# A row of c through TensorE, and the opening's vector work shared out anew, in a one-core encoder layer

## The chip, the cores and the metric

The kernel runs on one core of a Trainium2 chip. The metric is the device time of one execution in microseconds, given as the median over runs; before the change it is 1217.26 us (three runs, 1215.96 to 1217.44). One further execution was profiled. All work is in float32; the large products use pairs of fp32r numbers, a high part and a rest, and take three matrix products each.

## The reference

One layer of an encoder trunk over x (1024 rows, width 1024), with a condition vector c (1024):

```
mod = silu(c) @ w_ada + b_ada                       # six vectors of 1024
h   = rmsnorm(x) * norm_mix_w * (1 + sc_m) + sh_m
P   = h @ w_in                                      # z, xbc, dt, q, k, v
x   = x + g_m * (concat(ssd(z, xbc, dt), attention(q, k, v)) @ w_out)
h   = rmsnorm(x) * norm_ffn_w * (1 + sc_f) + sh_f
x   = x + g_f * conv_ffn(h)
out = rmsnorm(x)
```

rmsnorm(x) is x * (mean(x^2) + 1e-6)^(-1/2) for each row. silu(c) is c * sigmoid(c), computed as 0.5c * (1 + tanh(0.5c)). This case concerns only the first three lines, for the first 768 columns of w_in that the kernel treats (q, k and v of the first two pairs of heads).

## The kernel before

The opening loads eight tiles of x, 128 rows each, in two halves of four (hh = 0 and 1), and treats the width of h in eight blocks of 128 (kt = 0 to 7).

- c comes as a [128, 1024] array in which every row is c. It is loaded whole into rowa (L120), and its silu is made on all 128 partitions, by VectorE, ScalarE and VectorE (L191 to L193).
- Each x tile goes through norm1 (L296): ScalarE squares it and sums the rows (L268, into a scratch tile "junk" of one buffer), GpSimd adds epsilon and takes the power -1/2 (rstd, L116 and L117), and VectorE scales the tile in place (L301). Tiles 0 to 3 are loaded at once; tiles 4 to 7 are loaded from inside the loop over kt, behind a one-column copy on VectorE (L345) that depends on the scale of block kt (XL = 3, 4, 5, 6).
- In the first pass (hh = 0) each block kt needs its scale and shift. mod_col (L131) loads 128 rows of the transposed w_ada and VectorE multiplies them with rowa and sums (L134, "reduction"), once for the scale and once for the shift. mod_scale (L200) then makes the block's scale amix from two one-column instructions (L202, L204); mod_shift (L207) makes the shift bmix from one (L208).
- The block's weights (128 by 768) are loaded into one of two buffers (raws); ScalarE rounds them to a high part wsh and VectorE makes the rest wsl (split, L80; L85, L86).
- h_block (L270) makes the block's part of h: TensorE transposes four x tiles into PSUM (L273), ScalarE applies scale and shift into a float32 tile tmp (named hf, L276), VectorE rounds it to the high part hi (named hH, L277) and makes the rest lo (hL, L278).
- TensorE multiplies block kt into four accumulators for q and k (first_qk, L307, through mm3, L75: high by high L76, rest by high L77, high by rest L78) and two for v (first_v, L312; "vps"). Blocks 0 to 5 go in at once, blocks 6 and 7 in a tail after the loop, each product in a fixed order (those matmuls appear under L58). In that tail the first two blocks of the second half of x are transposed too.
- The second pass (hh = 1) uses the same weights again; it needs x tiles 4 to 7, no more reductions and no more weights.

Each engine issues its instructions in an order that a planner fixes when the program is built, from durations that it assumes; nothing is reordered at run time, so an instruction that waits holds back all behind it on its engine. DMAs are issued from SyncE's queue, also in order. The reductions' data have two buffers for the scale and two for the shift, the weights two: each load waits for the reduction or the weight rest two blocks earlier.

Of the kernel before, what the change touches and what calls it, by code (L numbers as in the profile page):

```python
# [10 lines left out]
F32 = mybir.dt.float32  # L11
F32R = mybir.dt.float32r
AF = mybir.ActivationFunctionType
ALU = mybir.AluOpType
PSUM = bass.MemoryType.PSUM

P = 128
D = 1024
# [6 lines left out]
EPS = 1e-6  # L25
# [9 lines left out]
B_ADA, NMIX, NFFN, SNW, SCW, SCB, FCW, DTB, ALOG, DSK = (  # L35
    0, 48, 56, 64, 68, 100, 108, 240, 248, 256)
NPK = 264
SH_M, SC_M, G_M, SH_F, SC_F, G_F = (8 * i for i in range(6))
# [26 lines left out]
def tile_block(ctx: ExitStack, tc: tile.TileContext, x, crep, pk, w_ada, w_first, w_ft, w_z,  # L65
               w_out, w_up, w_down, bias, fnw, out, dbg=None):
    nc = tc.nc
    V, A, T = (InOrder(tc, e) for e in (nc.vector, nc.scalar, nc.tensor))
    G = nc.gpsimd
# [19 lines left out]
    const = ctx.enter_context(tc.tile_pool(name="const", bufs=1))  # L89
    rw = ctx.enter_context(tc.tile_pool(name="rw", bufs=1, reuse_waits="tile"))  # L90
    es_l = ExitStack()
    wu = es_l.enter_context(tc.tile_pool(name="wu", bufs=2, reuse_waits="tile"))
    dram = ctx.enter_context(tc.tile_pool(name="dram", bufs=1, space=bass.MemoryType.DRAM))

    pkt = const.tile([P, 272], F32, name="pkt")[:, 0:NPK]
    rows_ = rw.tile([P, 2, D], F32, tag="w0", name="rows")
    rowa, rowb = rows_[:, 0, :], rows_[:, 1, :]
    raws = rw.tile([P, 2, D], F32, tag="w1", name="raws")
    ident = const.tile([P, P], F32, name="ident")
    mhalf = const.tile([P, 8], F32, name="mhalf")  # L100
    modc = const.tile([P, 48], F32, name="modc")
# [4 lines left out]
    def stat(n=1):  # L106
        if stc[0] + n > 64:
            stc[0] = 0
        a = st1[:, stc[0]:stc[0] + n]
        stc[0] += n  # L110
        return a

    def rstd(ms, eps=EPS):
        n = ms.shape[-1]
        r = stat(n)
        G.tensor_scalar(ms, ms, eps, 1.0, op0=ALU.add, op1=ALU.mult)  # L116
        G.tensor_tensor(r, ms, mhalf[:, 0:n], ALU.pow)  # L117
        return r

    nc.sync.dma_start(rowa, crep)  # L120
    nc.sync.dma_start(pkt, pk)
    make_identity(nc, ident)
    G.memset(mhalf, -0.5)
# [45 lines left out]
    def c4(ap):  # L169
        return ap.rearrange("p (a b) -> p a b", a=4)  # L170
# [11 lines left out]
    s0 = es_0.enter_context(tc.tile_pool(name="s0", bufs=1, side="right"))  # L182
    ps0b = es_0.enter_context(tc.tile_pool(name="ps0b", bufs=1, space=PSUM, side="right"))
    es_0a = ExitStack()
    ps0 = es_0a.enter_context(tc.tile_pool(name="ps0", bufs=1, space=PSUM))
# [2 lines left out]
        return qkp.tile([P, 1024], dt, tag="qk", name="qk")  # L188


    V.tensor_scalar(rowb, rowa, 0.5, None, op0=ALU.mult)  # L191
    A.activation(rowa, rowb, AF.Tanh)
    V.scalar_tensor_tensor(rowa, rowa, 1.0, rowb, op0=ALU.add, op1=ALU.mult)  # L193

    amix = const.tile([P, 16], F32, name="amix")[:, 0:8]
    bmix = const.tile([P, 8], F32, name="bmix")
# [3 lines left out]
    def mod_scale(dst, sc, nw, kt, n=1):  # L200
        t = stat(n)
        V.tensor_tensor(t, modc[:, sc + kt:sc + kt + n], pkt[:, B_ADA + sc + kt:B_ADA + sc + kt + n],  # L202
                        ALU.add)
        V.scalar_tensor_tensor(dst[:, kt:kt + n], t, 1.0, pkt[:, nw + kt:nw + kt + n],  # L204
                               op0=ALU.add, op1=ALU.mult)
# [6 lines left out]
    A.activation(na, pkt[:, ALOG:ALOG + 8], AF.Exp)  # L212
    V.tensor_scalar(pkt[:, SNW:SCW], pkt[:, SNW:SCW], 512.0 ** 0.5, None, op0=ALU.mult)


    qk = {}

# [52 lines left out]
    def h_block(hh, kt):  # L270
        tps = ps0.tile([P, 512], F32, tag="tp0", bufs=2, name="tp0")
        for j in range(4):
            T.transpose(tps[:, j * P:(j + 1) * P], xts[4 * hh + j][:, kt * P:(kt + 1) * P], ident)  # L273
        tmp = s0.tile([P, 512], F32, tag="hf", bufs=2, name="hf")
        hi, lo = ht(hh, kt)
        i = A.activation(tmp, tps, AF.Identity, scale=amix[:, kt:kt + 1], bias=bmix[:, kt:kt + 1])  # L276
        V.tensor_copy(hi, c4(tmp))  # L277
        return i, V.tensor_tensor(lo, c4(tmp), f32(hi), ALU.subtract)  # L278

    wsh = s0.tile([P, KT, 768], F32R, name="wsh")  # L280
# [7 lines left out]
    xts = []  # L288
# [7 lines left out]
    def norm1(st):  # L296
        ms = stat()
        junk = s0.tile([P, D], F32, tag="junk", name="junk")
        norm_to(xts[st], junk, ms)
        r = rstd(ms)  # L300
        V.tensor_scalar(xts[st], xts[st], r, None, op0=ALU.mult)  # L301

    for st in range(4):
        norm1(st)
# [24 lines left out]
    for hh in range(2):  # L329
        accs = [(ps0, ps0b)[n // 2].tile([P, 512], F32, tag="acc0", bufs=2, name="acc0") for n in range(4)]  # L330
        vps = [psv.tile([P, 2, 256], F32, tag=t, bufs=1, name="vps") for t in ("acc", "pv")]
        split_at = KT - (2, 4)[hh]
        tail = range(split_at, KT)
        for kt in range(KT):
            if hh == 0:
                mod_col(SC_M + kt, wu.tile([P, 1024], F32, tag="wh", name="adat"))
                mod_scale(amix, SC_M, NMIX, kt)
                mod_col(SH_M + kt, adw[:, kt % 2, :])
                mod_shift(bmix, SH_M, kt)
                t = raw_tile(768)  # L340
                nc.sync.dma_start(t, w_first[kt])
                split(wsh[:, kt, :], ws_lo(kt), t, A, V)
                for st in range(4, NT):
                    if XL[st - 4] == kt:
                        V.tensor_copy(xts[st][:, 0:1], amix[:, kt:kt + 1])  # L345
                        nc.sync.dma_start(xts[st], x[st * P:(st + 1) * P, :])
                        norm1(st)
            if hh == 0 or kt > 1:
                i = h_block(hh, kt)
            if hh == 1 and kt == 3:  # L350
                wpin = i
            if kt < split_at:
                for n in range(4):
                    first_qk(accs[n], n, hh, (kt,))
                first_v(vps, hh, (kt,))
        T.on, T.last = True, None
        if hh == 0:
            for kt in range(2):
                T.on = False
                h_block(1, kt)  # L360
                T.on = True
            first_v(vps, 0, tail)
            evac_v(vps, 0)
            for n in range(4):
                first_qk(accs[n], n, 0, tail)
                if n < 3:
                    evac_qkv(n // 2, n % 2, 0, accs[n], None, None)
            k1 = s0.tile([P, 512], F32, name="k1")
            A.activation(k1, accs[3], AF.Copy)
        else:  # L370
            for n in range(4):
                first_qk(accs[n], n, 1, tail)
                if n == 3:
                    es_0a.close()
                    ps1 = es_p1.enter_context(tc.tile_pool(name="ps1", bufs=1, space=PSUM,
                                                           reuse_waits="tile"))
                    s00 = scores(0, 0)
                    first_v(vps, 1, tail)
                evac_qkv(n // 2, n % 2, 1, accs[n], None, None)
            evac_v(vps, 1)  # L380
            evac_qkv(1, 1, 0, k1, None, None)
        T.on = False
# [207 lines left out]
    for ft in range(4):  # L590
        xt = bcp.tile([P, S], F32, tag="rm", bufs=2, name="xst")
        conv_mods(4 + ft, conv_silu(ft, xt))
        for hh in range(2):
            tps = tp_tile()
# [580 lines left out]
    t1, t2, t3, t4, b22 = (hr[n][:, :, c] for n in ("b11", "t2", "b12", "b21", "b22"))  # L1175
# [72 lines left out]
    bufs = {}  # L1248
# [97 lines left out]
    junk = [t[:, j, :] for t, j in ((xs, 2), (xs, 3), (xs, 4), (xs, 5), (ya, 6), (ya, 7))]  # L1346
# [219 lines left out]
```

## Time and profile before

| | |
|---|---|
| median of three runs | 1217.26 us (1215.96 to 1217.44) |
| profiled execution: its time, its span | 1219.3 us, 1217.5 us |
| TensorE busy, share of the span | 1170.7 us, 96% |
| VectorE | 928.7 us, 76% |
| ScalarE | 598.1 us, 49% |
| GpSimd | 148.6 us, 12% |
| mean granted TensorE clock | 0.991 |

The profile names engines PE (TensorE), PEld (its weight loads), DVE (VectorE), ACT (ScalarE), POOL (GpSimd) and SP (SyncE). A row in order of time gives the start in us, the duration, the engine, the line, the operation and the tiles; in brackets stands how long the engine had been idle and what ended that. A row for a stretch gives its length and, for each engine, the busy time with the number of instructions, and then the granted clock of TensorE, the DMAs' share and GB/s. A duration in a row runs to the end of the instruction; the next one on the same engine can start a little before that, and a row "x4" merges four.

### The profile page before, as it was taken

Reading aid. Unit: us, or ns where it says so; the run is one execution under the profiler, and the core shown is the slowest. Engines: PE = TensorE matmul, PEld = TensorE weight load, DVE = VectorE, ACT = ScalarE, POOL = GpSimd, SP = SyncE. Lnnn points to the kernel's source line nnn. Section 1 sums busy time; section 2 is a strip of 40 time slices with the busy share of each in tenths; the row PEclk is TensorE's granted clock in tenths of the full one; section 3 lists DMA queues with packets and bytes.
Section 4 is the critical chain, followed back from the end, with each engine's and each line's share of the span. In section 5 each row is a group of like instructions: output and inputs, shape, how many; then the busy total and the mean of one; then the engine's idle time right before and its main releaser. Section 6 shows DMA issues by size and latency. Waiting matters only on the chain.

```text
span 1217.5 us, 15642 instructions
## 1 busy us (share of the span) xinstructions
PE 1170.7 (96%) x5802; PEld 977.2 (80%) x5802; DVE 928.7 (76%) x1394; ACT 598.1 (49%) x1001; POOL 148.6 (12%) x174
## 2 busy tenths in 40 slices
PE   5998999989999999999999999999999999999996
PEld 3877887878788978888878888888888888888885
DVE  7846455686696678746999988988889869756986
ACT  4636454674333766676644533344334445433444
POOL 1202242440000134200000000000000000000522
PEclk9999999999999989999999999999999999999999
DMA  9612121311576201141223223322232277734443
GB/s 343 249 57 80 42 70 39 123 48 50 173 261 206 88 14 39 53 150 58 70 96 112 104 95 130 126 76 85 104 130 95 87 277 274 270 120 130 149 137 146
DMA packets 56395, 150.86 MB, mean 124 GB/s; under 512 B 5632, under 2 KB 5760, under 8 KB 54912
## 3 DMA queue, kind: packets, MB, share of 16 engines
q1 hardware_dynamic: 49264, 125.49, 30.5%
q10 hardware_dynamic: 7056, 24.38, 5.0%
q8 instruction: 45, 0.74, 0.2%
q14 instruction: 30, 0.25, 0.1%
HBM read 116.56 MB, written 29.10 MB: 120 GB/s over the span
## 4 chain that ended last, share of the span: by engine, by line
PE 70%; DVE 5%; ACT 1%; issue 1%; DMA 1%; POOL 0%; POOLq 0%; DVEq 0%; ACTq 0%; SPq 0%
PE wops L699 6%; PE dn L78 5%; PE dn L77 5%; PE dn L76 5%; PE uY L76 5%; PE uY L78 5%; PE uY L77 4%; PE uX L78 3%; PE uX L76 3%; PE uZ L77 3%; PE uZ L76 3%; PE uX L77 3%; PE uZ L78 3%; PE s L76 3%; PE s L77 3%; PE s L78 3%
## 5 line engine op out<-in xcount | busy, mean ns | idle before, releaser
L77 PE MATMUL dn<-w 128*128 128x512 f32 x296 | 108.1, 391 | 0.0
L76 PE MATMUL dn<-w 128*128 128x512 f32 x296 | 108.1, 391 | 0.0
L78 PE MATMUL dn<-w 128*128 128x512 f32 x296 | 100.2, 391 | 0.2 <-DVE w L86 0.2
L76 PE MATMUL uY<-tH,w 128*128 128x512 f32 x248 | 97.2, 392 | 0.0
L77 PE MATMUL uY<-tL,w 128*128 128x512 f32 x248 | 97.0, 391 | 0.0
L78 PE MATMUL uY<-tH,w 128*128 128x512 f32 x248 | 96.9, 391 | 0.0
L1427 POOL TENSOR_TENSOR ya<-ya,xs 128x512 f32<-128x512 f32 x4 | 17.2, 4338 | 557.7 <-ACT xs L1423 557.7
L85 ACT ACTIVATE w<-ya 128x1024 fp32r<-128x1024 f32 (+1 forms) x41 | 39.2, 956 | 87.3 <-PE uY L78 84.2
L699 PE MATMUL wops<-hH,yhl 128*128 128x512 f32 x224 | 75.9, 407 | 2.9 <-DVE yhl L86 1.5
L78 PEld LDWEIGHTS dn<-w 128*128 128x128 f32 x296 | 55.4, 188 | 13.2 <-DVE w L86 1.1
L76 PEld LDWEIGHTS dn<-w 128*128 128x128 f32 x296 | 55.5, 188 | 12.4
L77 PEld LDWEIGHTS dn<-w 128*128 128x128 f32 x296 | 55.5, 188 | 12.2
L413 DVE CUSTOM_DVE_ANT_0 p<-s,bias 128x640 f32<-128x640 f32 (+4 forms) x64 | 40.7, 652 | 25.0 <-PE tp L445 9.0
L85 ACT ACTIVATE w<-xs 128x1024 fp32r<-128x1024 f32 (+1 forms) x41 | 39.1, 953 | 37.3 <-PE uY L78 33.3
L419 POOL TENSOR_SCALAR p<-p,st 128x640 f32<-128x640 f32 (+4 forms) x64 | 46.1, 726 | 76.7 <-DVE st L418 66.5
L86 DVE TENSOR_TENSOR pt<-tp,pt 128x512 fp32r<-128x512 f32 (+2 forms) x72 | 42.0, 595 | 16.9 <-ACT pt L85 16.5
L78 PEld LDWEIGHTS uY<-tH,w 128*128 128x128 f32 x248 | 46.6, 188 | 10.4
L76 PEld LDWEIGHTS uY<-tH,w 128*128 128x128 f32 x248 | 46.6, 188 | 10.4
L77 PEld LDWEIGHTS uY<-tL,w 128*128 128x128 f32 x248 | 46.6, 188 | 10.2
L699 PEld LDWEIGHTS wops<-hH,yhl 128*128 128x128 f32 x224 | 42.9, 193 | 12.5 <-DVE yhl L86 1.9
L76 PE MATMUL s<-hH,wh 128*128 128x512 f32 x128 | 50.2, 392 | 1.6 <-DVE ct L520 1.6
L1101 DVE SCALAR_TENSOR_TENSOR a<-cv,pkt,a 128x1023 f32<-128x1023 f32 (+1 forms) x40 | 50.9, 1276 | 0.1
(459 smaller groups left out, 3430.5 us busy)
## 6 DMA issues: line engine op xcount, KB each, us to landing
wos<-in_w_ada_dram SPq DMA_DIRECT2D x25, 512.0 KB, 4.7
gz<-a ACTq DMA_DIRECT2D x10, 1024.0 KB, 4.9
ya<-in_w_up_dram SPq DMA_DIRECT2D x11, 768.0 KB, 4.2
xs<-in_w_up_dram SPq DMA_DIRECT2D x11, 768.0 KB, 4.1
adat<-in_w_ada_dram SPq DMA_DIRECT2D x16, 512.0 KB, 5.7
raws<-in_w_ft_dram SPq DMA_DIRECT2D x14, 512.0 KB, 3.7
gy<-a ACTq DMA_DIRECT2D x10, 512.0 KB, 2.6
qk<-in_x_dram SPq DMA_DIRECT2D x8, 512.0 KB, 6.4
```

The costliest lines, as they stand in the source:

```text
L76: T.matmul(ps, lh, rh, start=start, stop=False, skip_group_check=more)
L77: T.matmul(ps, lh, rl, start=False, stop=False, skip_group_check=more)
L78: T.matmul(ps, ll, rh, start=False, stop=stop, skip_group_check=more)
L85: i = A.activation(hi, src, AF.Copy) if ehi is A else ehi.tensor_copy(hi, src)
L86: return i, elo.tensor_tensor(lo, src, f32(hi), ALU.subtract)
L413: V.tensor_tensor_reduce(out=dst, in0=src, in1=bsl, scale=-1.0, scalar=3e38, op0=ALU.add, op1=ALU.min, accum_out=nm)
L419: G.tensor_scalar(pv_, pv_, rr, 1.0, op0=ALU.mult, op1=ALU.mult)
L699: i = op(*a, **k)
L1101: V.scalar_tensor_tensor(a[:, j:S], c[:, 0:S - j], w[2 - j], a[:, j:S], op0=ALU.mult, op1=ALU.add)
L1427: G.tensor_tensor(src, src, fnr[:, halves[1]], ALU.mult)
```

## The change

Four edits, all in the opening.

1. Only one row of c is loaded, into one partition. Its silu is made there, by the same three instructions on one partition. Two matmuls with a row of 128 ones spread it over the 128 partitions into two PSUM tiles, and ScalarE copies these into rowa. The tanh result lies in the junk tile, the ones in one of the two buffers that the scale reductions' data use.
2. In h_block, for the first half of x only (hh = 0), ScalarE writes hi itself, straight from PSUM, ahead of tmp; VectorE no longer rounds tmp.
3. x tiles 3 to 7 are scaled by ScalarE; tiles 0 to 2 stay with VectorE. Epsilon is added by VectorE; GpSimd keeps only the power.
4. The block's scale is made by one VectorE instruction instead of two, from a table am1 = (b_ada + 1) * norm_mix_w that is made once.

```
-    nc.sync.dma_start(rowa, crep)
+    nc.sync.dma_start(rowa[0:1], crep[0:1, :])
...
-    V.tensor_scalar(rowb, rowa, 0.5, None, op0=ALU.mult)
-    A.activation(rowa, rowb, AF.Tanh)
-    V.scalar_tensor_tensor(rowa, rowa, 1.0, rowb, op0=ALU.add, op1=ALU.mult)
+    c1, t1 = rowb[0:1], s0.tile([P, D], F32, tag="junk", name="t1")
+    ones1 = wu.tile([P, 1024], F32, tag="wh", name="ones1")[0:1, 0:P]
+    G.memset(ones1, 1.0)
+    V.tensor_scalar(c1, rowa[0:1], 0.5, None, op0=ALU.mult)
+    A.activation(t1[0:1], c1, AF.Tanh)
+    V.scalar_tensor_tensor(c1, t1[0:1], 1.0, c1, op0=ALU.add, op1=ALU.mult)
+    for j in range(2):
+        ps = ps0.tile([P, 512], F32, tag="tp0", bufs=2, name="crow")
+        T.matmul(ps, ones1, c1[:, 512 * j:512 * j + 512], start=True, stop=True)
+        A.activation(rowa[:, 512 * j:512 * j + 512], ps, AF.Copy)
...
+    am1 = const.tile([P, 8], F32, name="am1")
+    V.scalar_tensor_tensor(am1, pkt[:, B_ADA + SC_M:B_ADA + SC_M + 8], 1.0, pkt[:, NMIX:NMIX + 8],
+                           op0=ALU.add, op1=ALU.mult)
...
-        i = A.activation(tmp, tps, AF.Identity, scale=amix[:, kt:kt + 1], bias=bmix[:, kt:kt + 1])
-        V.tensor_copy(hi, c4(tmp))
+        ab = dict(scale=amix[:, kt:kt + 1], bias=bmix[:, kt:kt + 1])
+        if hh == 0:
+            A.activation(hi, c4(tps), AF.Identity, **ab)
+        i = A.activation(tmp, tps, AF.Identity, **ab)
+        if hh:
+            V.tensor_copy(hi, c4(tmp))
...
-        r = rstd(ms)
-        V.tensor_scalar(xts[st], xts[st], r, None, op0=ALU.mult)
+        r = stat()
+        V.tensor_scalar(ms, ms, EPS, None, op0=ALU.add)
+        G.tensor_tensor(r, ms, mhalf[:, 0:1], ALU.pow)
+        if st < 3:
+            V.tensor_scalar(xts[st], xts[st], r, None, op0=ALU.mult)
+        else:
+            A.activation(xts[st], xts[st], AF.Copy, scale=r)
...
-                mod_scale(amix, SC_M, NMIX, kt)
+                V.scalar_tensor_tensor(amix[:, kt:kt + 1], modc[:, SC_M + kt:SC_M + kt + 1],
+                                       pkt[:, NMIX + kt:NMIX + kt + 1], am1[:, kt:kt + 1],
+                                       op0=ALU.mult, op1=ALU.add)
```

With it the planner orders the opening's instructions anew on every engine; from the second pass on the order stays as it was but for a few neighbours. On ScalarE the new order is: squares 0 and 1, first copy of c's row, squares 2 and 3, second copy, scaling of tile 3, weights 0, high part and tmp 0, and so on to block 5; then square of tile 4, high part and tmp 6, square 5, scaling of tile 4, weights 6 and 7, scaling of tile 5, square 6, high part and tmp 7, square 7, scalings of tiles 6 and 7, and the evacuations. On VectorE the epsilon additions stand in the same order and wait there for ScalarE's squares.

## The prediction

> **What bounds the kernel now.** First the page's head, busy table and chain; then stretches of the opening, since the edits end there; then that stage in order of time, engine by engine.
>
> ```profile
> span 1217.5 us, 15642 instructions
> PE 1170.7 (96%) x5802; PEld 977.2 (80%) x5802; DVE 928.7 (76%) x1394; ACT 598.1 (49%) x1001; POOL 148.6 (12%) x174
> PE 70%; DVE 5%; ACT 1%; issue 1%; DMA 1%; POOL 0%; POOLq 0%; DVEq 0%; ACTq 0%; SPq 0%
> ```
> ```profile
> 10.00:20.00 10.00, 4.43 (x13) 2.65 (x14) 8.47 (x18) 4.33 (x7) 3.25 (x5) 1.00 1.02 405
> 20.00:30.00 10.00, 10.00 (x58) 8.83 (x58) 10.00 (x24) 3.15 (x4) 0.00 (x0) 1.00 0.94 342
> 40.00:50.00 10.00, 9.06 (x54) 7.71 (x54) 9.39 (x24) 6.25 (x10) 3.88 (x4) 1.00 0.82 323
> ```
>
> TensorE carries the span. In 10 to 20 us it is half idle; from 20 us TensorE and VectorE are both full, while ScalarE has room. The columns are TensorE, its weight loads, VectorE, ScalarE, GpSimd, the granted clock, DMA share and GB/s. So the time that this change can move is when the first matmuls start and how often TensorE waits until its stream through the first half of the rows is done.
>
> ```profile
> 18.75 2.08 PE L76 MATMUL acc<-hH,wsh 128*128 128x512 f32 x4 [0.37 <-DVE hH L277]
> 24.42 1.18 PE L76 MATMUL acc<-hH,wsh 128*128 128x512 f32 x4
> 45.54 0.51 PE L77 MATMUL acc<-hL,wsh 128*128 128x512 f32 x1 [0.55 <-DVE hL L278]
> 50.10 0.39 PE L58 MATMUL vps<-wsh,hH 128*128 128x256 f32 x1 [0.49 <-DVE hH L277]
> 50.82 0.38 PE L58 MATMUL vps<-wsh,hL 128*128 128x256 f32 x1 [0.22 <-DVE hL L278]
> 58.80 1.03 PE L273 MATMUL tp<-ident,qk 128*128 128x128 f32 x8
> ```
>
> TensorE starts on block 0 at 18.75, on block 1 at 24.42, waits 0.55, 0.49 and 0.22 us, uses the low part of block 7 at 50.82, and then runs 8.0 us without a wait to 58.80. What comes later hangs on TensorE's progress, so **a lead at block 7's low part is what reaches the end**.
>
> **The change part by part.** Rows of VectorE and ScalarE, from which the durations come (duration in column two; the next instruction starts a little before it ends):
>
> ```profile
> 4.47 0.69 DVE L191 TENSOR_SCALAR rows<-rows 128x1024 f32<-128x1024 f32 x1 [4.47 <-DMA rows<-in_crep_dram]
> 6.29 1.22 DVE L193 SCALAR_TENSOR_TENSOR rows<-rows 128x1024 f32<-128x1024 f32 x1 [1.04 <-ACT rows L192]
> 12.52 1.22 DVE L134 CUSTOM_DVE_ANT_0 adat<-adat,rows 128x1024 f32<-128x1024 f32 x1
> 14.18 0.75 DVE L301 TENSOR_SCALAR qk<-qk,st 128x1024 f32<-128x1024 f32 x1 [0.43 <-POOL st L117]
> 14.91 1.22 DVE L134 CUSTOM_DVE_ANT_0 adat<-adat,rows 128x1024 f32<-128x1024 f32 x1
> 16.06 0.15 DVE L204 SCALAR_TENSOR_TENSOR amix<-st,pkt 128x1 f32<-128x1 f32 x1
> 18.27 0.42 DVE L277 CAST hH<-hf 128x512 fp32r<-128x512 f32 x1
> 18.61 1.22 DVE L134 CUSTOM_DVE_ANT_0 adat<-adat,rows 128x1024 f32<-128x1024 f32 x1
> 19.82 0.68 DVE L278 TENSOR_TENSOR hL<-hf,hH 128x512 fp32r<-128x512 f32 x1
> 20.43 0.15 DVE L208 TENSOR_TENSOR bmix<-modc,pkt 128x1 f32<-128x1 f32 x1
> 20.57 0.95 DVE L86 TENSOR_TENSOR wsl<-raws,wsh 128x768 fp32r<-128x768 f32 x1
> 21.43 1.22 DVE L134 CUSTOM_DVE_ANT_0 adat<-adat,rows 128x1024 f32<-128x1024 f32 x1
> 39.86 0.15 DVE L204 SCALAR_TENSOR_TENSOR amix<-st,pkt 128x1 f32<-128x1 f32 x1
> 50.08 0.69 DVE L278 TENSOR_TENSOR hL<-hf,hH 128x512 fp32r<-128x512 f32 x1
> ```
> ```profile
> 5.20 1.06 ACT L192 ACTIVATE rows<-rows 128x1024 f32<-128x1024 f32 x1 [0.16 <-DVE rows L191]
> 10.84 1.06 ACT L268 ACTIVATE junk<-qk 128x1024 f32<-128x1024 f32 x1
> 11.80 0.19 ACT L268 ACTIVATION_READ_ACCUMULATOR junk<-qk 128x1 f32 x1
> 14.32 0.84 ACT L85 ACTIVATE wsh<-raws 128x768 fp32r<-128x768 f32 x1 [2.33 <-DMA raws<-in_w_first_dram]
> 57.29 1.45 ACT L276 ACTIVATE hf<-tp,bmix,amix 128x512 f32<-128x512 f32 x2
> ```
>
> From start to next start on VectorE: a reduction L134 1.15 (14.91 to 16.06), the cast L277 0.34, a rest L278 0.61, a weight rest L86 0.86, a one-column instruction 0.07, an x scaling L301 0.7. On ScalarE: a square 1.15 with its read, a tmp (L276) 0.7, weights' high parts 0.75, and by the square 1.0 for scaling an x tile.
>
> *c as one row.*
>
> ```profile
> rows<-in_crep_dram SPq DMA_DIRECT2D x1, 512.0 KB, 3.7
> ```
>
> The load falls from 512 KB to 4 KB; at 405 GB/s what is queued behind lands up to 1.3 us earlier (weights at about 13.0, not 14.3). On one partition the three instructions keep their 1024 columns, so their 0.69, 1.06 and 1.22 stay. The row cannot land after the present 4.47; without its 1.3 us of transfer it lands near 3.1, which I take. So silu(c) is ready at 3.1 + 0.69 + 1.06 + 1.22 = 6.1, before 7.5.
>
> *Spreading it.* Two matmuls and two ScalarE copies are new. The nearest rows are the ones that spread gates later:
>
> ```profile
> L144 PE MATMUL rowps<-gt,tle x8: 590/591/592, 384.7 to 394.8; 128*128 128x512 f32 x8
> L145 ACT ACTIVATE rows<-rowps x3: 598/598/600, 385.7 to 395.4; 128x512 f32<-128x512 f32 x3
> ```
>
> The matmuls fall in TensorE's idle start: nothing. The copies stand in ScalarE's built order between squares 2 and 3 and behind square 4. The first square cannot precede 6.1 (tanh's result lies in the squares' scratch tile), so the spread row is ready at 6.1 + 4 x 1.15 + 2 x 0.6 + handoffs = 12.2. That replaces the 12.52 at which the first reduction starts.
>
> *Epsilon on VectorE, the fourth x tile on ScalarE.* Now GpSimd's two instructions per tile are one; eight columns of 0.07 come onto VectorE. The power's price depends on VectorE:
>
> ```profile
> 11.27 0.55 POOL L117 TENSOR_TENSOR st<-st,mhalf 128x1 f32<-128x1 f32 x1
> 12.73 1.41 POOL L117 TENSOR_TENSOR st<-st,mhalf 128x1 f32<-128x1 f32 x1
> ```
>
> 1.41 beside a reduction, 0.55 beside none. The changed power for tile 3 would start at 12.0, just ahead of the reduction: I take 0.55; the other end is behind one or two reductions, 1.15 to 2.3 later, which VectorE's whole chain follows. With 1.15 the gain below is gone (1217.4). The Trainium skill (SBUF — State Buffer, "SBUF: two separate sides") says that whichever of a GpSimd instruction and a VectorE one with two SBUF inputs starts first holds the shared ports to its end. The trace agrees (1.41 against 0.55); by it the end with 1.15 holds if the reduction comes first, and mine if the power does.
>
> The second reduction no longer stands behind the fourth scaling: 13.4, before 14.91. Shift and scale follow at 14.6. ScalarE meanwhile scales tile 3 (12.6 to 13.6) and makes block 0's weights (to 14.4), then writes block 0's high part to 15.4. **Block 0's matmuls start at 15.5 instead of 18.75.** Both starts run slow: four matmuls took 2.08 us there and 1.18 at 24.42.
>
> *Block 1.* Built order on VectorE from 14.6: weight rest 0.86 (held to 14.9 by ScalarE), reduction, rest, shift, weight rest, two reductions, two scales: 14.9 + 0.86 + 1.15 + 0.61 + 0.07 + 0.86 + 2.3 + 0.14 = 20.9, ScalarE 0.8 more: block 1 starts at 21.7, not 24.42. Lead 2.7.
>
> *VectorE to block 5's scale.* From 12.2: 13 reductions 14.95, six weight rests 5.2, five rests 3.05, sixteen columns 1.1, waits about 0.9: 37.4. Before, 39.86: lead 2.5. No cast and no second one-column step per block is in it.
>
> *ScalarE's tail gives it back.* ScalarE's built order behind that scale is: high part and tmp 5 (1.4), square of tile 4 (1.15), high part and tmp 6 (1.4), square 5 (1.15), scaling of tile 4 (1.0), weights 6 (0.75), 6.9 us: 44.3. VectorE's order holds weight rest 6 behind it (0.86), then reduction (1.15), rest of weights 7 (0.86), scale 7: 47.3. High part 7 is done at 48.1, tmp at 48.9, low part at 49.6 to 49.8 (handoffs). Before, 50.08 + 0.69 = 50.77. **Lead 1.0 at the step that counts.** TensorE, ahead by 2.7 at block 1 and without its old 1.26 of waits, waits here for about 3 us. These waits come out of its lead, not on top.
>
> *Behind it.* The last two scalings hold ScalarE's evacuation of vps to about 52.5; by the same order the third accumulator is free at 60.5, and TensorE wants it at 61.2, so 0.7 covers this.
>
> Sum: 1.0 us. The profiled execution took 1219.3 (span 1217.5 and 1.8 around it), so 1218.3; its median of runs is 1217.26, 2.0 below it, so **1216.3**.
>
> **The rivals.** *The tail does not wait (faster).* If ScalarE's squares and scalings fit in shorter gaps, TensorE keeps the 2.7 and saves its 1.26: 2.7 to 4.0, 1213.3 to 1214.6. For it: ScalarE was busy 6.25 of 10 us at 40 to 50. Against it: the order makes VectorE wait for weights 6 behind a square and a scaling, and engines issue in order.
>
> *The wait lowers TensorE's clock (slower).*
>
> ```profile
> 104.94 0.33 PE L445 MATMUL tp<-ident,p 128*128 128x128 f32 x1 [0.72 <-POOL p L419]
> ```
> ```profile
> 104.00:106.00 2.00, 1.27 (x7) 0.73 (x6) 1.34 (x7) 1.24 (x6) 0.89 (x3) 1.00 0.00 0
> 106.00:108.00 2.00, 1.72 (x5) 1.43 (x6) 1.47 (x7) 1.41 (x5) 1.12 (x3) 0.60 0.00 0
> 108.00:110.00 2.00, 2.00 (x9) 1.71 (x8) 1.42 (x6) 1.91 (x5) 0.59 (x1) 0.55 0.00 0
> ```
>
> After a stretch in which TensorE was busy 1.27 of 2 us the clock was 0.60 and 0.55 for 4 us: 1.7 us lost. My 3 us of waiting at 45 to 50 is worse than that. One such drop gives 1216.3 + 1.7 = 1218.0; a second, or one on a lead already spent by the slow power (1.15), 1219.2 to 1219.7. It decides against the change from 1.0 us lost upward. Against it: 40 to 50 was 9.06 busy and kept 1.00. The Trainium skill (TensorE: Matmul & The Clock Gate, "Part 1: The HAM clock gate") wants about 3.4 us of idleness first; by that no drop and 1216.3. The rows differ: the longest gap before the 0.60 was the 0.72 above.
>
> *It does not do what it says:* if the DMAs' landing, not their size, holds the start, ScalarE's 12.2 stands anyway, as it hangs on 4 squares.
>
> **How the numbers follow.** Under 0.2% (2.4 us) a measurement of this kernel tells little from no change. Given-back lead 0.46 (1214.9 to 1217.5, nearly all within; 0.12 of it with the slow power, 1217.4); no wait 0.32 (all faster); clock drop 0.22, of which 0.12 is slower by over 0.2%. Faster 0.34, same 0.54, slower 0.12. The range, 1213.2 to 1219.0, cuts about 0.1 at each side; the likeliest case's own is 1214.9 to 1217.5.
>
> **What would show it.** Right: first reduction near 12.2 and second near 13.4; first L76 near 15.5; no idle between the two; VectorE waiting for ScalarE's weights 6 near 43 to 44; TensorE's longest wait before block 7 at 46 to 48. Wrong: a power above 1 us for tile 3; a granted clock under 1.00 in 46 to 54; or a low part 7 before 48.5, which would mean that ScalarE's tail is shorter than its rows.

## The result and the profile after

The changed kernel takes 1220.82 us (median of seven, 1219.91 to 1225.52) beside 1216.60 for the kernel before (seven, 1213.82 to 1217.66). The ratio is 1.0037, with a 95% interval of 1.0021 to 1.0053: **slower by about 4.5 us (2.6 to 6.4)**, outside the predicted range, where 1216.3 and no measurable difference had been forecast. The profiled execution took 1220.08 us with a span of 1218.3.

The page's head for the changed kernel, to set beside the same lines of before:

```profile
span 1218.3 us, 15657 instructions
PE 1176.8 (97%) x5806; PEld 979.2 (80%) x5806; DVE 924.3 (76%) x1382; ACT 608.3 (50%) x1016; POOL 142.3 (12%) x167
```

VectorE lost 4.4 us of work and ScalarE gained 10.2, as the edits say. But TensorE is busy for 6.1 us more, with four more instructions out of 5,802: the spread of c explains the four instructions and 3.75 us of it (its row below), in TensorE's idle start, and no lost time. The place to look at is TensorE's pace.

First the opening, VectorE and GpSimd in order of time:

```profile
2.28 0.68 DVE L194 TENSOR_SCALAR rows<-rows 1x1024 f32<-1x1024 f32 x1 [2.28 <-DMA rows<-in_crep_dram]
11.44 1.23 DVE L134 CUSTOM_DVE_ANT_0 adat<-adat,rows 128x1024 f32<-128x1024 f32 x1
12.59 1.22 DVE L134 CUSTOM_DVE_ANT_0 adat<-adat,rows 128x1024 f32<-128x1024 f32 x1
37.63 0.22 DVE L357 SCALAR_TENSOR_TENSOR amix<-modc,pkt,am 128x1 f32<-128x1 f32 x1
44.61 0.96 DVE L86 TENSOR_TENSOR wsl<-raws,wsh 128x768 fp32r<-128x768 f32 x1 [1.55 <-ACT wsh L85]
49.29 0.69 DVE L293 TENSOR_TENSOR hL<-hf,hH 128x512 fp32r<-128x512 f32 x1 [1.51 <-ACT hf L290]
```
```profile
11.48 1.59 POOL L317 TENSOR_TENSOR st<-st,mhalf 128x1 f32<-128x1 f32 x1 [0.93 <-DVE st L316]
```

and TensorE, with the stretch in which it waits for block 7:

```profile
5.44 3.75 PE L199 MATMUL crow<-rows,ones 1*128 1x512 f32 x4 [5.44 <-DVE rows L196]
...
15.70 2.08 PE L76 MATMUL acc<-hH,wsh 128*128 128x512 f32 x4 [0.71 <-ACT hH L289]
...
48.64 0.39 PE L58 MATMUL vps<-wsh,hH 128*128 128x256 f32 x1 [1.40 <-ACT hH L289]
50.03 0.39 PE L58 MATMUL vps<-wsh,hL 128*128 128x256 f32 x1 [0.29 <-DVE hL L293]
```
```profile
46.00:48.00 2.00, 1.24 (x11) 1.01 (x9) 1.78 (x5) 1.58 (x4) 0.14 (x1) 1.00 0.55 180
48.00:50.00 2.00, 0.94 (x4) 0.50 (x4) 0.69 (x1) 2.00 (x3) 0.40 (x1) 1.00 0.71 238
50.00:52.00 2.00, 1.97 (x16) 1.97 (x17) 0.15 (x1) 2.00 (x4) 0.55 (x1) 1.00 0.31 121
```

Between these two executions the opening did what it was forecast to do: TensorE uses the low part of block 7 at 50.03 instead of 50.82, a lead of 0.8 us, at a clock of 1.00. (Further executions of either opening, below, put the lead nearer 0.4.) Matched matmul by matmul, the changed kernel is still 0.6 us ahead at 68 us. At 98 us it is level.

The larger loss lies where the change touches nothing. A view of one tile's instructions gives, for each group, the least, median and longest duration in ns and the starts of the first and the last one. Three groups of before:

```profile
L58 PE MATMUL acc<-hH,wsl x24: 388/388/475, 53.3 to 91.1; 128*128 128x512 f32 x24
L76 PE MATMUL uY<-tH,w x248: 387/392/398, 598.0 to 989.4; 128*128 128x512 f32 x124
L76 PE MATMUL dn<-w x296: 387/392/398, 995.6 to 1199.1; 128*128 128x512 f32 x148
```

and of after:

```profile
L58 PE MATMUL acc<-hH,wsl x23: 392/393/479, 53.2 to 90.8; 128*128 128x512 f32 x23
L76 PE MATMUL uY<-tH,w x248: 387/392/400, 595.5 to 988.9; 128*128 128x512 f32 x124
L76 PE MATMUL dn<-w x296: 387/393/401, 995.2 to 1199.8; 128*128 128x512 f32 x148
```

From its first to its last start the group into uY took 391.4 us before and 393.4 after, the group into dn 203.5 and 204.6. TensorE is full there in both (300.00 of 300 us between 700 and 1000, at a clock of 1.00), with 1309 matmuls in those 300 us before and 1301 after. **The same matmuls run 0.6% slower, 3.1 us over the feed-forward stage**, and about 0.7 us more is lost from the opening to 98 us. Together 3.8, less the lead of 0.8: 3.0 us, inside the measured 2.6 to 6.4.

Between the two kernels TensorE's instructions in that stage are the same in the same order, and only six places in the order of ScalarE and VectorE differ; what differs throughout is addresses. am1 is a new constant of 8 float32 in each partition, 32 bytes. The constants lie at the lower end of the memory, and all that is allocated on that side after them moves up by the same amount. In the built programs, byte addresses in a partition:

```
                      rows (later w tiles)   hH (later tH)       wh
before                3520                   36288               28096, 32192
after                 3552                   36320               24032, 19936
```

3520 and 36288 are multiples of 64; 3552 and 36320 are 32 past one. The tiles on the upper side (wsh, qk, b11h, xs) are where they were in steps of 64. Of the five buffers that the w tiles of the feed-forward stage take in turn, three lie on the left side and two on the upper one, where they did not move. (The buffers of wh and wl, next to each other on the left, changed places too, since the row of ones takes one of wh's first, and wsh moved by 4096.)

### The profile page after: what moved, and what is told of

It reads as the page before. It is cut to its first block, busy times and chain, and to the rows that moved or that the text cites. A ratio compares the mean times of both kernels' runs of the same rounds, so it can differ in the third digit from the quotient of the medians.

```text
span 1218.3 us, 15657 instructions
## 1 busy us (share of the span) xinstructions
PE 1176.8 (97%) x5806; PEld 979.2 (80%) x5806; DVE 924.3 (76%) x1382; ACT 608.3 (50%) x1016; POOL 142.3 (12%) x167
## 4 chain that ended last, share of the span: by engine, by line
PE 71%; DVE 5%; ACT 1%; DMA 1%; issue 0%; POOL 0%; POOLq 0%; DVEq 0%; ACTq 0%; SPq 0%
PE wops L721 6%; PE dn L78 6%; PE dn L77 6%; PE dn L76 6%; PE uY L78 5%; PE uY L77 5%; PE uY L76 5%; PE uX L78 3%; PE uZ L77 3%; PE uX L77 3%; PE uZ L76 3%; PE uX L76 3%; PE uZ L78 3%; PE s L76 3%; PE s L77 3%; PE s L78 3%
## 5 line engine op out<-in xcount | busy, mean ns | idle before, releaser
L85 ACT ACTIVATE w<-xs 128x1024 fp32r<-128x1024 f32 (+1 forms) x41 | 39.1, 954 | 37.4 <-PE uY L78 33.8
L438 ACT ACTIVATE p<-p,st 128x640 f32<-128x640 f32 (+4 forms) x64 | 44.1, 690 | 14.4 <-DVE st L435 14.2
```

The source lines that it names most:

```text
L85: i = A.activation(hi, src, AF.Copy) if ehi is A else ehi.tensor_copy(hi, src)
L438: A.activation(pv_, pv_, AF.Exp, scale=-1.0, bias=nm, accum_out=rs)
```

## The experiments

The theory **P** (place): the slower pace comes from where the operands lie, and am1's 32 bytes moved them. Against it **O** (opening): the new order of the opening, or what it leaves in queues, slows what follows. A table of the mean time from one matmul's start to the next, in ns, in five groups of 512-column matmuls (worked out from the starts in each trace, gaps left out), serves for several runs. "Shift" is how far the left-side tiles lie from their place in the kernel before, in bytes (for w, the three of its buffers that lie on that side). The name right behind the arrow is the operand that is streamed (512 columns), the second the one that is loaded (128 by 128): hH, tH and b11h are streamed, wsh, wh and w are loaded, and in dn both are w tiles. wsh and b11h lie on the other side and are not shifted. (The expectations for e6 and e7 below have loaded and streamed the wrong way round.)

```
run                 shift of h,  w    acc<-hH,wsh  s<-hH,wh  uY<-tH,w  uX<-b11h,w  dn<-w
before                       0   0      230.2        227.8     229.0     231.1      229.1
after                       32  32      233.9        228.3     230.7     232.1      230.7
e1_am1_64                   64  64      232.0        228.2     229.9     230.9      229.7
e2_gap32                    32  32      233.4        228.3     230.6     232.0      230.7
e3_gap64                    64  64      232.0        227.9     230.1     231.0      229.7
e5_am1_in_na                 0   0      230.1        228.1     229.1     231.1      229.2
e6_h_32                     32   0      234.4        233.1     233.6     231.3      229.1
e7_w_32                     64  32      232.0        233.0     233.0     232.2      230.7
e8_gap128                  128 128      233.5        228.2     230.9     230.0      229.3
e9_tile4_vector              0   0      229.9        227.8     229.1     231.2      229.2
```

### The whole change, with am1 padded to 64 bytes

```
-    am1 = const.tile([P, 8], F32, name="am1")
+    am1 = const.tile([P, 16], F32, name="am1")[:, 0:8]
```

> The whole change stays; only the new constant am1 takes 64 bytes of each partition instead of 32, so that every tile behind it on the left side (rows, the w tiles, hH, hL, tH, tL) begins on a multiple of 64 bytes again, as in the kernel before. Theory P (place): the slower pace of the feed-forward stage comes from tiles that begin 32 bytes off a multiple of 64; the 512-column matmuls go back from about 231 to about 229.5 ns from start to start, and what is left is the lead of the opening, 0.8 us: 0.3 to 1.5 us under the kernel before, ratio 0.9988 to 0.9998. Theory O (opening): the new order of the opening, or what it leaves on the queues, is what slows the rest; it is all still there, so the time stays 4 to 5 us over the kernel before, ratio 1.0033 to 1.0041, and the pace stays at 231 ns.

Measured: 1219.69 (twelve runs), ratio 1.0021 (1.0007 to 1.0035). Neither theory's number. The pace came back in part: dn from 230.7 to 229.7 where before has 229.1, tH to 229.9, and b11h wholly. So 64 bytes cost less than 32, but not nothing: being a multiple of 64 is not the whole rule.

### The kernel before, with an unread constant of 32 or of 64 bytes

```
     na = const.tile([P, 16], F32, name="na")[:, 0:8]
+    gap = const.tile([P, 8], F32, name="gap")        # second run: [P, 16]
+    G.memset(gap, 0.0)
```

> The kernel before with nothing changed but a constant of 32 bytes of each partition, filled once by GpSimd and read by nobody, behind na. Theory P: all that the change lost comes with it, without any lead to set against it: 4 to 5.5 us slower than the kernel before, ratio 1.0033 to 1.0045, pace of the 512-column matmuls about 231 ns. Theory O: none of the opening is changed, so the time is that of the kernel before, within 1 us, pace 229.5 ns.

> The kernel before with the same unread constant at 64 bytes instead of 32. Theory P: the left-side tiles begin on multiples of 64 bytes as before, so the time is that of the kernel before, within 1 us, pace 229.5 ns. A rival within it, theory S (any shift of the tiles moves them to other places than those the kernel was built around): slower by 4 us or more, as with 32 bytes. Theory O: the time of the kernel before.

Measured: 1.0055 (1.0035 to 1.0075) with 32 bytes and 1.0013 (1.0003 to 1.0024) with 64. The tile view of the kernel with 32:

```profile
L76 PE MATMUL uY<-tH,w x248: 387/392/399, 596.9 to 990.3; 128*128 128x512 f32 x124
L76 PE MATMUL dn<-w x296: 387/393/400, 996.6 to 1201.2; 128*128 128x512 f32 x148
```

393.4 and 204.6 us from first to last, the changed kernel's figures to the tenth, with no edit of the opening at all. Theory O falls: an unread 32-byte constant reproduces the slow pace. With 64 bytes 1.4 us are lost against before from 650 us to the end, matched matmul by matmul (3.3 with 32), the same as with am1 at 64. The theory that any shift costs the same falls too, since the price depends on the shift. The run with 32 bytes costs 6.7 us (4.3 to 9.1), more than the 3.8 that its pace explains; a lower granted clock goes with most of the rest (see the longer wait, below).

### The whole change, with am1 in free space

na's tile has 16 columns, of which the kernel uses 8. With am1 in the other eight nothing on that side moves.

```
-    na = const.tile([P, 16], F32, name="na")[:, 0:8]
+    na16 = const.tile([P, 16], F32, name="na")
+    na = na16[:, 0:8]
...
-    am1 = const.tile([P, 8], F32, name="am1")
+    am1 = na16[:, 8:16]
```

> The whole change, with am1 in the unused upper half of na's 64 bytes, so that no tile behind it on the left side moves at all against the kernel before. Theory P (place): the 512-column matmuls of the feed-forward stage run at the pace of the kernel before, 229.1 ns for those into dn and 229.0 for tH (the change: 230.7 and 230.7), and what is left is the lead of the opening, 0.8 to 1.3 us: ratio 0.9988 to 0.9995, 1215.0 to 1216.0 beside 1216.5. Theory R (remainder): the change also gives the w tiles of the pool wu another order, and moves wsh by 4096 bytes; if that, not the place of am1, is what costs, the pace stays at 230 ns or more and the time stays 1.5 us or more above the kernel before.

Measured: ratio 1.0001 (0.9988 to 1.0014), median 1217.67 beside 1216.14; five runs lie at 1213.3 to 1215.8 and seven at 1217.6 to 1219.0. Every group is back at the pace of before, within 0.3 ns; matched matmul by matmul the distance to before stays at 1.86 us from 650 to 1110 us. So the order of the buffers and wsh's 4096 bytes cost nothing in pace, and theory R falls. The interval covers the expected gain of 0.8 and also none. Its profiled execution shows one thing that the changed kernel's did not, in TensorE's wait for block 7 and the stretches around it:

```profile
49.22 0.38 PE L58 MATMUL vps<-wsh,hH 128*128 128x256 f32 x1 [1.90 <-ACT hH L290]
```
```profile
46.00:48.00 2.00, 1.32 (x12) 1.11 (x10) 2.00 (x4) 1.97 (x3) 0.00 (x0) 1.00 0.30 41
48.00:50.00 2.00, 0.61 (x3) 0.41 (x4) 0.49 (x4) 1.61 (x3) 0.55 (x1) 1.00 0.89 258
50.00:52.00 2.00, 1.71 (x11) 1.47 (x12) 0.72 (x2) 2.00 (x4) 0.55 (x1) 0.84 0.58 229
52.00:54.00 2.00, 2.00 (x10) 1.92 (x9) 0.53 (x1) 1.61 (x3) 0.00 (x0) 0.50 0.03 8
54.00:56.00 2.00, 2.00 (x9) 1.56 (x8) 0.85 (x2) 0.69 (x2) 0.00 (x0) 0.81 0.00 0
```

TensorE waited 1.90 us for block 7's high part, was busy 1.93 of the 4 us from 46 to 50, and its clock then fell to 0.50: the second rival of the prediction, in one execution. (In the changed kernel's it was busy 2.18 of those 4 us, and kept 1.00.)

### Which operand's place

```
 e6:  +    hgap = es_l.enter_context(tc.tile_pool(name="hgap", bufs=1))     # ahead of pool htp
      +    G.memset(hgap.tile([P, 8], F32, name="gp2"), 0.0)
 e7:  the same, and the 32-byte constant behind na
 e8:  the constant behind na alone, [P, 32]
```

> The kernel before with an unread 32-byte tile just ahead of hH, so that only hH, hL, tH, tL and the dn tiles in their place begin 32 bytes off a multiple of 64; rows, raws, wh, wl and the w tiles stay. If it is the place of the weights loaded for the matmuls (tH, tL are the loaded operand, w is the 512-column one): the matmuls on tH and tL slow by 1.6 ns (229.0 to 230.7) and those on b11h, b21h and t1h, and those into dn, stay at 231.1 and 229.1; about 1.8 us slower. If it is the place of the 512-column operand w: no group slows, 0 within 1 us. If both count: part in each.

> The kernel before with the unread 32-byte constant behind na and a second one ahead of hH, so that rows, raws, wh, wl and the w tiles in their place begin 32 bytes off a multiple of 64, while hH, hL, tH, tL lie 64 bytes on, on a multiple of 64. If the 512-column operand w decides: all groups of the feed-forward stage slow as with the whole shift (dn 229.1 to 230.7, b11h 231.1 to 232.1), 3.5 to 5 us slower. If the loaded operand decides: only the tH and tL groups move, by the 1.0 ns they showed under the shift of 64, 1 to 2 us slower.

> The kernel before with the unread constant at 128 bytes. The kernel before has its left-side tiles at 64 bytes past a multiple of 128; a shift of 64 still cost 1.4 us of pace in the feed-forward stage and 32 cost 3.3. If what counts is the place within 128 bytes: 128 brings back the pace of the kernel before (dn 229.1, tH 229.0), time within 1 us. If any move away costs: dn at 229.7 or more, 1.5 to 4 us slower.

Measured: 1.0076 (1.0060 to 1.0092), 1.0091 (1.0077 to 1.0105) and 1.0045 (1.0030 to 1.0060). **Operands moved by 32 bytes against each other cost more than both moved together.** The groups of the run in which h alone moved:

```profile
L78 PE MATMUL s<-hH,wl x128: 389/396/484, 267.5 to 372.4; 128*128 128x512 f32 x128
L76 PE MATMUL uY<-tH,w x248: 388/394/399, 597.3 to 993.1; 128*128 128x512 f32 x124
L76 PE MATMUL dn<-w x296: 387/392/398, 999.4 to 1202.9; 128*128 128x512 f32 x148
```

uY took 395.8 us from first to last (391.4 before), dn 203.5 as before. What counts is how the two operands of a matmul lie to each other: s<-hH,wh takes 228 ns wherever both have the same shift (0, 32, 64, 128) and 233 where they differ by 32, whichever of them moved. The feed-forward stage shows the same once its matmuls are sorted by buffer, since a shift of the left side moves three of w's buffers and not the other two. For dn (left and upper side; distance is streamed start minus loaded start in bytes, modulo 256):

```
streamed, loaded        distance          ns from start to start
                      before  after          before   after
left, left                 0      0           227.9   228.7
left, upper               64     96           229.0   233.2
upper, left              192    160           233.3   234.3
upper, upper               0      0           227.2   228.6
```

And for all such fp32r matmuls (into acc, s, wops, uX, uY, uZ and dn) of all fourteen kernels, by that distance alone:

```
distance                               0      32      64      96     128     160     192
mean, ns                           228.3   233.2   229.7   233.3   232.6   234.0   233.2
lowest mean of a group in a run    226.7   232.9   227.6   231.5   231.3   233.5   232.8
highest                            230.0   233.6   231.4   236.9   233.1   234.6   233.7
```

Distances of 0 and 64 are fast, the others slow, in the first stage, the attention projections and the feed-forward stage alike; 224 did not occur. acc<-hH,wsh fits too: hH and wsh are 64 apart before, and 96, 128 and 192 with h moved by 32, 64 and 128. With these means the feed-forward stage would lose 2.8 us in the change, 1.4 with a shift of 64, 4.7 with h alone moved, 5.6 in e7 and nothing (-0.2) with a shift of 128; matched matmul by matmul it lost 3.1, 1.3, 4.5, 5.4 and 0.6. The means come from the same traces, so this shows that they fit, not that they foretell. They are not the whole: the pairs of upper buffers went from 227.2 to 228.6 though neither moved, and why stays open.

My expectation for e6, that only the groups on tH and tL slow in the feed-forward stage, by 1.6 ns, had the groups but not the size (4.6) and left out the stages before it. For e7, dn and b11h slowed as expected from a shift of w, which is their loaded operand, and tH slowed by 4.0.

The shift of 128 rules out a plain period of 128 bytes: dn came back, tH did not (230.9), and b11h became faster than before (230.0). Its pace explains only about 1.2 of its 5.5 us, and a lower granted clock goes with some 1.6; what the rest is stays open.

### x tiles by VectorE again

In the kernel with am1 at 64 bytes, VectorE scales tiles 4 to 7 (`if st != 3`).

> As the run with am1 at 64 bytes, but x tiles 4 to 7 are scaled by VectorE again, and only tile 3 by ScalarE. ScalarE's chain at the end of the opening (weights, scale of x, high part, one behind the other) loses its four scales; VectorE takes them back, where it had about 1.5 us idle ahead of the last rest of the weights. If ScalarE's tail is what gave the lead back, the last low part comes earlier than 49.3 and the lead at the last matmuls of x grows from 0.8 to between 1.2 and 2.5 us: 1 to 2.5 us under the kernel before by theory P, ratio 0.998 to 0.9992. If VectorE is the bound instead, the lead is 0.8 us or less. By theory O it is still 3 to 5 us over the kernel before.

Measured: 1.0015 (1.0003 to 1.0027). TensorE used the last low part at 50.29, a lead of 0.5; 49.57 with ScalarE scaling. From the first reduction to there it took 38.98 us, 38.44 with ScalarE scaling; in time the two runs cannot be told apart (1.0015 and 1.0021). VectorE becomes the bound: it waits 0.44 to 0.66 us for each of GpSimd's powers, here with a reduction queued behind.

```profile
41.01 0.76 DVE L319 TENSOR_SCALAR qk<-qk,st 128x1024 f32<-128x1024 f32 x1 [0.66 <-POOL st L317]
41.68 1.22 DVE L134 CUSTOM_DVE_ANT_0 adat<-adat,rows 128x1024 f32<-128x1024 f32 x1
```

### One tile to VectorE

With am1 in na's half, VectorE scales tile 4 and ScalarE tiles 3 and 5 to 7, so that ScalarE's weights 6 and 7 move up.

```
+        if st == 4:
+            late.append(lambda: V.tensor_scalar(xts[st], xts[st], r, None, op0=ALU.mult))
```

> am1 in na's free half, and x tile 4 scaled by VectorE instead of ScalarE (tiles 3, 5, 6 and 7 stay on ScalarE). On ScalarE the weights 6 and 7 stood behind that scale (43.28 to 44.32 in the run before), and VectorE waited 1.55 us for weights 6. Theory T (ScalarE's tail holds block 7): the last low part comes 0.5 to 0.9 us earlier than without it, TensorE's wait for block 7's high part falls from 1.3 to 1.9 us to about 1, and the time is 0.5 us under that of the run with am1 in na: ratio to the kernel before 0.9990 to 1.0000. Theory V (VectorE holds it, as when it took all four tiles): the last low part comes at the same time or later, ratio 1.000 to 1.001. Theory K (the wait at block 7 is what lowers TensorE's clock in part of the executions): with the shorter wait the mean granted clock rises from 0.993 to 0.994, that of the kernel before.

Measured: median 1214.32 (twelve), **ratio 0.9983 (0.9972 to 0.9995): faster than both kernels**, by about 2.1 us (0.6 to 3.4) against before. Its ScalarE, VectorE and TensorE:

```profile
42.23 1.58 ACT L85 ACTIVATE wsh<-raws 128x768 fp32r<-128x768 f32 x2
```
```profile
11.13 1.22 DVE L134 CUSTOM_DVE_ANT_0 adat<-adat,rows 128x1024 f32<-128x1024 f32 x1
...
43.36 1.82 DVE L86 TENSOR_TENSOR wsl<-raws,wsh 128x768 fp32r<-128x768 f32 x2
```
```profile
47.66 0.39 PE L58 MATMUL vps<-wsh,hH 128*128 128x256 f32 x1 [0.59 <-ACT hH L290]
49.05 0.38 PE L58 MATMUL vps<-wsh,hL 128*128 128x256 f32 x1 [0.29 <-DVE hL L294]
```

Both weight rests follow without the 1.55 us of waiting, TensorE's wait for block 7 is 0.59 instead of 1.40, and the lead is 1.77. Theory T holds: ScalarE's tail held block 7. (The tail is about 0.5 us shorter by it, 37.92 against 38.45 us from the first reduction on in the table below; the rest of the 1.77 is this execution's early first reduction. The mean granted clock is 0.994, 0.993 with am1 in na alone.)

### The parts of the opening

Both with am1 in na's half, one execution each (1215.48 and 1214.78 us, from which no difference in time follows):

```
 e10:  c loaded, halved, tanh and product on 128 partitions, as in the kernel before
 e11:  i = A.activation(tmp, ...); V.tensor_copy(hi, c4(tmp))    for both halves, as in the kernel before
```

> am1 in na's free half, and the handling of c put back as before (128 rows loaded, halved, tanh and product on all partitions); the rest of the change stays. One look at the opening: the first reduction moves from 11.4 back to about 12.5. If all of the opening hangs on that reduction, the scale of block 5 and the last low part come 1.1 us later than in the change (38.7 and 50.4) and the lead of the opening falls from 0.8 to about 0 or below. If the tail is held by the arrival of x tiles 4 to 7 instead, the last low part stays near 49.3 and the spreading of c by TensorE is worth nothing at the end.

> am1 in na's free half, and block 0 to 7's high parts copied by VectorE again (0.42 us each) instead of written by ScalarE (0.67 to 0.78 each); the rest of the change stays. One look at the opening: up to block 5's scale VectorE has five or six copies more, so that scale comes at 39.7 to 40.2 instead of 37.6. If ScalarE's tail is the limit behind it, ScalarE is freed of three high parts there, 2.0 us, and the last low part comes at 49 to 49.6, no later than in the change; if VectorE is, it comes 2 to 3 us later, 51 to 52, and the high parts by ScalarE are what the whole lead hangs on.

The start of the first reduction, of the scale of block 5, and of TensorE's matmul on the last low part, with the way from the first to the last:

```
                        first reduction   scale 5   last low part   first to last
before                      12.52          39.86       50.82           38.30
after                       11.44          37.63       50.03           38.59
e1_am1_64                   11.13          37.17       49.57           38.44
e5_am1_in_na                12.17          38.22       50.62           38.45
e4_x_by_vector              11.31          37.37       50.29           38.98
e9_tile4_vector             11.13          37.18       49.05           37.92
e10_c_as_before             12.39          35.17       50.50           38.11
e11_high_by_vector          11.54          38.72       50.28           38.74
e2, e3, e6, e7, e8         11.73          39.08       50.00           37.91
  (before's opening)    to 12.41       to 39.76    to 50.91        to 38.62
```

After the first reduction the opening takes the same time in both, 37.9 to 38.6 us in six executions of before's and 38.4 to 38.6 in three of the change's. So what lead there is lies in the first reduction's start, and that goes back to 12.39 with c handled as before (where the planner also orders the blocks otherwise, so scale 5 comes early). The high parts by ScalarE bring block 5's scale 1.1 us nearer to the first reduction (26.2 against 27.2 us) and ScalarE's tail takes that back (12.4 against 11.6 behind it): worth nothing at the end. The start itself differs by 0.8 us between executions of before's opening (11.73 to 12.52, mean 12.20) and by 1.0 in the seven that treat c in the new way (11.13 to 12.17, mean 11.42, with 11.22 in the run below). The last low part is used at 50.44 on the mean of six and at 50.07 on that of three. So the lead of 0.8 between two executions is within this scatter, some 0.4 is the better estimate, and one execution of e10 or e11 does not show a time to a few tenths.

### A longer wait for block 7

With am1 in na's half, ScalarE writes block 7's high part four times instead of once.

> am1 in na's free half, and ScalarE writes block 7's high part four times instead of once (the same values), which makes TensorE's wait for it longer by about 2.0 us, to 3.3 to 3.9 us. Theory K (waits here lower TensorE's clock): the granted clock falls to 0.5 to 0.85 for some 4 us between 50 and 57 in the profiled execution and in nearly all others; mean clock of the runs 0.992 or less, and the time 2 us by the wait and 1.5 to 2 us by the clock above that of the run with am1 in na. Against it: the clock stays at 1.00 between 46 and 60, mean 0.993, and only the 2 us of the wait are added, less what TensorE has in hand behind it.

Measured: 1.0041 (1.0027 to 1.0055); mean granted clock of its seven runs 0.990, and 0.993 without the longer wait. The planner put squares and scalings between the four writes, so that the wait grew by more than the 2 us expected:

```profile
50.34 0.33 PE L285 MATMUL tp<-ident,qk 128*128 128x128 f32 x1 [3.55 <-ACT qk L323]
52.04 0.48 PE L285 MATMUL tp<-ident,qk 128*128 128x128 f32 x1 [1.38 <-ACT qk L323]
53.52 0.58 PE L58 MATMUL vps<-wsh,hH 128*128 128x256 f32 x1 [1.00 <-ACT hH L291]
```
```profile
50.00:52.00 2.00, 0.33 (x1) 0.14 (x1) 0.00 (x0) 2.00 (x4) 0.06 (x1) 0.84 0.20 80
52.00:54.00 2.00, 0.96 (x3) 0.66 (x3) 0.00 (x0) 1.97 (x3) 0.00 (x0) 0.50 0.00 0
54.00:56.00 2.00, 2.00 (x11) 1.83 (x11) 1.79 (x3) 1.46 (x3) 0.00 (x0) 0.50 0.00 0
56.00:58.00 2.00, 2.00 (x11) 2.00 (x11) 1.78 (x4) 1.50 (x3) 0.00 (x0) 0.50 0.04 8
```

The clock fell to half for some 7 us: theory K's mechanism, a wait here that lowers the clock, works at this place. How much of the 5 us is the wait and how much the clock, this run does not separate. Nor do the runs show how often the drop comes in the change itself: of the four profiled executions with waits of 1.3 to 1.9 us (the change, am1 at 64 bytes, am1 in na, x tiles by VectorE) one has it, but the mean clocks do not follow the opening (0.992 in the change, 0.994 in before, and 0.992 and 0.995 in the two kernels with before's opening and a 32- or 64-byte constant).

The granted clock explains most of the scatter between runs: over the 160 runs of kernels that ran three times or more, a run with 0.001 less than its kernel's mean is 0.88 us longer. By that slope the means of the runs can be set side by side at equal clock. Against before (the 67 runs beside the experiments, 0.9939) the change is then 3.7 us slower (5.0 between the means as run, at 0.9924), e2 4.4 (6.5), e6 8.2, e7 9.1, e8 2.2 (3.8), e3 2.1 and e1 1.2; am1 in na is 1.2 faster and e9 1.8 faster. These are estimates, and why the runs of the change, e2 and e8 had a lower clock they do not say.

## Why the prediction was wrong, step by step

- **"What comes later hangs on TensorE's progress, so a lead at block 7's low part is what reaches the end": this step failed.** It took all that follows the opening as unchanged. The matmuls behind it run 0.4 to 1.6% slower in the two stages named, because the new constant moved the operands on one side by 32 bytes and with it changed their distance from those on the other: +3.8 us against a lead of 0.8. The prediction costed am1 as an instruction and not as an allocation; none of its rivals held it. A hint stood in the code: amix and na are allocated with 16 columns where 8 are used.
- *c as one row; spreading it.* Right in kind, too cautious in size: the row landed at 2.28 (3.1 forecast), the spread matmuls took 3.75 us of idle time, and the first reduction started at 11.44 (12.2 forecast, 12.52 before).
- *Epsilon and the fourth tile.* The power of tile 3 took 1.59, not the 0.55 that I chose: the other end of that bound. I had it start ahead of the first reduction; it started 0.04 us behind it and ended at 13.07, 0.48 behind the start of the second. The Trainium skill (SBUF — State Buffer, "SBUF: two separate sides") has whichever of the two starts first hold the shared ports to its end; the trace agrees in that the power was held up by the reduction that had just started (1.59 here, 0.55 for the three powers with no reduction beside them). That the second reduction kept its 1.22 with the power's last 0.48 beside it does not fit a port held to the end, unless the power's end in the profile is late. The earlier spread hid it: block 0 started at 15.70, 15.5 forecast.
- *Block 1, block 5's scale.* 22.75 and 37.63, against 21.7 and 37.4. Close, and without meaning for the end, as the next step says.
- *"ScalarE's tail gives it back".* Right: VectorE waited 1.55 us for weights 6 at 44.61, scale 7 came at 47.50 (47.3), the low part at 49.29, TensorE used it at 50.03 and led by 0.8 (1.0 forecast), though it stood idle for 1.8 of the 4 us from 46 to 50 and not for about 3. That the size came out so near is in part luck, as executions of one opening differ by 0.9 at that step (50.00 to 50.91). The runs put it more sharply: behind the first reduction nothing was gained at all (38.3 and 38.6 us), and with one scaling taken off ScalarE the kernel was faster than before (0.9983), which it was not shown to be with the four edits and am1 in na alone (1.0001).
- *Behind it, "0.7 covers this".* Right: TensorE ran on from 50.03 to 63 us without a wait.
- *The tail does not wait.* Did not happen.
- *The wait lowers TensorE's clock.* Not in the changed kernel's profile (1.00 from 46 to 60), so it is not what the trace of the change shows, but real: one of four profiled executions with this opening has it, and the longer wait brought it. The Trainium skill (TensorE: Matmul & The Clock Gate, "Part 1: The HAM clock gate") asks for an idle window of about 3.4 us; here the clock fell after 4 us in which TensorE was busy 1.93, with no gap above 1.90. So that page's rule did not hold as I had worked it out.

By pieces, −0.8 for the opening and +3.8 for the pace make +3.0 us of the measured 4.5 (2.6 to 6.4). The lower mean clock of its runs goes with another 1.3; whether the change or chance lowered it stays open.

## What to carry to other kernels

A new small tile is also an allocation. Before costing its instruction, list which tiles lie behind it, how far they move, and which matmuls take one operand that moves and one that stays; where a stage is bound by TensorE, half a per cent of its pace was worth more here than any wait in the opening. Put such a constant where nothing moves (a free half of a padded tile), and compare the start-to-start time of the same matmuls in an untouched stage before looking for a cause in the edit. When an in-order engine holds a chain's tail, take one instruction off it rather than speed up what feeds it.

## What the runs showed of the hardware

- The time of a 512-column fp32r matmul, start to start, went with the distance between the starts of its streamed and its loaded operand, modulo 256 bytes: on the mean 228.3 ns at 0, 229.7 at 64, and 232.6 to 234.0 at 32, 96, 128, 160 and 192, over the matmuls of fourteen kernels in the first stage, the attention projections and the feed-forward stage. What in the chip does this, no run here shows.
- An unread constant of 32 bytes made this kernel 0.55% slower, and one that moved h alone 0.76%.
- A GpSimd power on one column took 0.55 us with no reduction beside it and 1.46 to 1.59 where one had just started.
- TensorE's clock fell to half after 4 us with 1.93 us of work; with 2.18 it did not (one execution each).
- A run whose mean granted clock was 0.001 lower was 0.88 us longer, of some 1217.
